# Weight halves that GpSimd's DMAs read twice from DRAM, and a fifth seven-product pair in six units

## The chip, the cores and the metric

The kernel runs on one core of one Trainium2 chip. The metric is device time in microseconds (us). The kernel before takes 2133.17 us, the median of three runs (2133.06 to 2133.46). TensorE is called PE here, VectorE DVE, ScalarE ACT, GpSimd POOL and SyncE SP.

## The reference

Two layers of a decoder trunk on 256 tokens of width 2048, in float32:

```python
h = rms_norm(x, attn_norm)
proj = einsum('bsd,de->bse', h, w_in)          # 2048 x 6160, split into eight parts
o_gla = gated linear attention, chunks of 64, per-head norm, times silu(gate)
o_sb  = stick-breaking attention on normalised q, k, per-head norm
x = x + einsum('bse,ed->bsd', concat(o_gla, o_sb), w_o)       # 2048 x 2048
up = square(relu(einsum('bsd,df->bsf', rms_norm(x, mlp_norm), w_up)))   # 2048 x 8192
x = x + einsum('bsf,fd->bsd', up, w_down)                      # 8192 x 2048
```

## The kernel before, in words

Each product of two float32 numbers is made of three matmuls: an operand is split into a rounded high part and the rest, its low part, and `product` adds high x high, high x low and low x high in one PSUM bank. A weight tile is so turned into `whi` (ACT copies it, rounding, L1008) and `wlo` (DVE subtracts `whi` from the raw weights, L1012).

The MLP, the output projection and some columns of the input projection run in `ordered`, which cuts them into *units*. A unit of the kinds in `BIG` (up, down, and three parts of the input projection, iv, ik and iq) multiplies all 2048 rows of its operand by 1024 weight columns. It goes through eight *pairs* j = 0 to 7; a pair is 256 rows of weights, so 2 x 2 blocks of weights against 2 x 2 blocks of activations. There are 38 such units: for each of four quarters q of the hidden width, up with n2 = 0, up with n2 = 1, down with n2 = 0, down with n2 = 1, in each of the two layers, and iv, ik, iq before each layer's attention.

- An ordinary pair takes eight block products, in two steps: (banks 2, 4), then (banks 3, 8), 12 matmuls each.
- A *seven-product* pair (those in `FAST`, 1, 3, 5 and 6) follows Winograd's form of Strassen's method: seven block products, 21 matmuls, in four steps with the banks (2, 3), (5, 7), (1, 6) and (4). DVE first makes sums of weight blocks for it (`ts`, then two sums in place in `raw`, all at L840), and four low parts instead of two. Sums of the activation blocks come from `forms`.
- An *added* pair (`ADDED`, 2 and 7) is an ordinary pair whose low parts are not made by DVE: ACT writes the negated, rounded weights into a tile `dlo` (L1018), and a DMA of POOL's adds the raw weights, already in SBUF, to it (L1021). Its high parts are still made by ACT at L1008.

`STEPS` (L22) lists the steps of a unit by their pair; `FEWER` is for the one unit iv that follows a down unit. After the last steps of a unit, `sums` and `half` of `down_tail` or `up_tail` drain its banks on DVE. An up unit with n2 = 0 and q over 0 follows a down unit, so that no transposes stand in its first steps; a unit that follows an up unit has that unit's `turn` there, in the banks 5, 7, 1 and 6.

The raw weights of a pair, 1 MiB, are loaded by SP into one of `RAWS` = 5 tiles (`load`, L981; two loads by columns for pair 7, L976). `whi` has `RING` = 5 tiles, `wlo` `LOWS` = 4, `dlo` `ADDS` = 2.

The order on PE is the order in which `ordered` lists the steps. The order of DVE and ACT is written out ahead of time by `Plan.run`: each piece has a length and a due time, counted back from the PE piece that needs it, and a simulated engine always takes the ready piece that is due first. SP and POOL take their instructions in order. Nothing of that is decided on the chip: an engine waits at the first instruction that is not ready, with all behind it.

```python
STEPS = [0, 0, 1, 1, 1, 2, 3, 1, 3, 2, 3, 3, 4, 4, 5, 5, 6, 5, 5, 6, 6, 6, 7, 7]
FAST = (1, 3, 5, 6)
ADDED = (2, 7)
```

Of the kernel before, what the change touches and what calls it, by code (L numbers as in the profile page):

```python
# [17 lines left out]
P = 128  # L18
# [29 lines left out]
class Plan:  # L48
# [10 lines left out]
    class Piece:  # L59
        def __init__(self, engine, length, fn, deps, lag):  # L60
            self.engine, self.length, self.fn, self.lag = engine, length, fn, lag
            self.deps = deps
            self.users = []
            self.after = []
# [4 lines left out]
    def add(self, engine, length, fn, *deps, lag=0.0):  # L69
        flat = []  # L70
        for d in deps:
            flat.extend(d if isinstance(d, (list, tuple)) else [d])
        self.pieces.append(Plan.Piece(engine, length, fn, [d for d in flat if d], lag))
        return self.pieces[-1]

    def run(self):
# [25 lines left out]
        order, events, count = [], [], 0  # L102
        for p in self.pieces:
            if not p.deps:
                events.append((0.0, count, p))
                count += 1
        came = set()
        while events:
            now, _, p = heapq.heappop(events)
# [6 lines left out]
            for e in free:  # L116
                if free[e] > now + 1e-9:
                    continue
                if e in ready:
                    if not ready[e]:  # L120
                        continue
                    p = heapq.heappop(ready[e])[2]
# [6 lines left out]
                heapq.heappush(events, (free[e], count, None))  # L129
                count += 1  # L130
                for u in p.users:
# [4 lines left out]
                    if not left[u]:  # L136
                        heapq.heappush(events, (at[u], count, u))
# [9 lines left out]
def trunk_kernel(  # L147
# [59 lines left out]

    ATT = ("wg", "ident16", "mask16", "tri", "nones", "gmask", "reset", "v4", "lr", "lrT", "ha", "hh", "hl", "hA", "on", "dec", "S", "kdz", "row", "bc", "eg")
    MLP = ("whi5", "dlo", "sxh", "sx", "ts", "raw2")
# [213 lines left out]
    def forms(op, i, t, tag):  # L423

        keep = tag is None
# [16 lines left out]
        def high():  # L442
            if e:
                if keep:
# [378 lines left out]
    def ordered(l, units, hT, rst, ug, gates_t, mixed=None, ons=None):  # L823
# [11 lines left out]
        RING, LOWS, ADDS, RAWS = 5, 4, 2, 5  # L835
# [11 lines left out]
        def unit_order(u):  # L847

            kind, _, n2 = units[u]
            if kind == "g":  # L850
                return [i // 2 for i in range(8)], ()
            if kind == "o":
                pairs = ((4, 5, 6, 7, 0, 1, 2, 3), (4, 5, 6, 0, 7, 1, 2, 3))[n2]
                return [j for j in pairs for _ in range(4 if j < 2 else 2)], (0, 1)
            return FEWER if u and units[u - 1][0] == "down" and kind == "iv" else (STEPS, FAST)

        def step_banks(u, j, is_fast):
# [4 lines left out]
            if kind in BIG and j in ADDED and not by_columns(u, j):  # L862
# [24 lines left out]
        def squares(n, ss):  # L887
            return add("ACT", 2 * A1, lambda: norm_squares(n, ss), x_done[n])
# [23 lines left out]
        def made(f, got, tag_fast, first):  # L912
# [9 lines left out]
            if tag_fast:  # L922
                e = add("DVE", 1.25, lambda: part(0), first)
            b = add("ACT", A1 * (2 if tag_fast else 1), lambda: part(1), e)
            return add("DVE", 1.1 if tag_fast else V1, lambda: part(2), b)

        def turned(n, h2, m, op, key, ll, sums=False):
# [4 lines left out]
            if sums and fast(i):  # L932
                box = []
                b = add("ACT", A1, lambda: box.append(scaled()), a)
                free[m] = [b]
                return made(
                    lambda: forms(op, i, box[0], None if op is hT else "sxh"), None, True, b
# [23 lines left out]
        def load(u, i):  # L961
# [4 lines left out]
            def fn():  # L966
                if x % RAWS >= RAWS - 2:
                    box.append(tmp("raw2", [P, 2, 1024], bufs=2))
# [5 lines left out]
                if by_columns(u, i):  # L974
                    for c in range(2):
                        nc.sync.dma_start(  # L976
                            dst[:, c, :].rearrange("p (k n) -> p k n", k=2),
                            src[:, :, c * 512 : (c + 1) * 512],
                        )
                else:  # L980
                    nc.sync.dma_start(dst, src)  # L981
# [8 lines left out]
        def by_columns(u, i):  # L990

            return units[u][0] in BIG and i in ADDED and i == unit_order(u)[0][-1]
# [763 lines left out]
```

## Time and profile before

| | |
|---|---|
| median of three runs | 2133.17 us |
| the profiled execution: span | 2131.6 us |
| PE busy | 2123.5 us, 10094 matmuls |
| DVE busy | 1929.5 us (91%) |
| ACT busy | 1535.1 us (72%) |
| POOL busy | 152.1 us |
| HBM read | 405.12 MB |
| DMAs of SP's queue | 407.25 MB |
| DMAs of POOL's queue (the adds) | 79.70 MB |

The profiled execution's span, from the first to the last instruction, lies 1.6 us under the median of the runs; that is what a run has around it. In the rows below, "x" is a count, a tile's name stands as out<-in, and a window is given as start:end in us from the span's start. Busy time of an engine is the union of its instructions' times, and successive instructions of DVE and PE overlap a little in the records, so a sum of means is some per cent above it.

### The profile page before, as it was taken

Reading aid. Unit: us, or ns where it says so; the run is one execution under the profiler, and the core shown is the slowest. Engines: PE = TensorE matmul, PEld = TensorE weight load, DVE = VectorE, ACT = ScalarE, POOL = GpSimd, SP = SyncE. Lnnn points to the kernel's source line nnn. Section 1 sums busy time; section 2 is a strip of 40 time slices with the busy share of each in tenths; the row PEclk is TensorE's granted clock in tenths of the full one; section 3 lists DMA queues with packets and bytes.
Section 4 is the critical chain, followed back from the end, with each engine's and each line's share of the span. In section 5 each row is a group of like instructions: output and inputs, shape, how many; then the busy total and the mean of one; then the engine's idle time right before and its main releaser. Section 6 shows DMA issues by size and latency. Waiting matters only on the chain.

```text
span 2131.6 us, 28370 instructions
## 1 busy us (share of the span) xinstructions
PE 2123.5 (100%) x10094; PEld 1768.9 (83%) x10094; DVE 1929.5 (91%) x2598; ACT 1535.1 (72%) x1989; POOL 152.1 (7%) x210
## 2 busy tenths in 40 slices
PE   9999999999999999999999999999999999999999
PEld 7888888888888888888888888888888888888887
DVE  6988779999999999999998886799999999999998
ACT  7777666777677677677777665667876776776775
POOL 0010000000000000000000100000000000000000
PEclk9999999999999999999999999999999999999999
DMA  8975355688888888878888644657888888888886
GB/s 287 265 203 182 115 198 178 217 242 264 249 247 252 249 256 249 269 237 254 238 260 252 178 138 136 201 186 219 262 234 267 245 261 250 246 254 248 254 252 178
DMA packets 156114, 488.76 MB, mean 229 GB/s; under 512 B 9690, under 2 KB 18466, under 8 KB 155972
## 3 DMA queue, kind: packets, MB, share of 16 engines
q1 hardware_dynamic: 134084, 407.25, 55.9%
q0 software_dynamic: 21888, 79.70, 19.7%
q8 instruction: 79, 1.29, 0.2%
q14 instruction: 63, 0.52, 0.1%
HBM read 405.12 MB, written 2.10 MB: 191 GB/s over the span
## 4 chain that ended last, share of the span: by engine, by line
PE 96%; DVE 2%; ACT 1%; issue 0%; DMA 0%; DVEq 0%; ACTq 0%
PE acc L594 3%; PE acc L596 3%; PE acc L595 3%; DVE wlo L1012 0%; PE ps L1693 0%; PE ps L1686 0%; DVE wlo L577 0%; PE ps L705 0%; PE ps L1643 0%; PE ps L759 0%; PE ps L723 0%; DMA dlo<-raw 0%; DVE t L1548 0%; PE ps L471 0%; PE ps L771 0%
## 5 line engine op out<-in xcount | busy, mean ns | idle before, releaser
L1008 ACT ACTIVATE whi<-raw 128x1024 fp32r<-128x1024 f32 (+1 forms) x847 | 814.9, 976 | 344.5 <-issue 48.2
L1012 DVE TENSOR_TENSOR wlo<-raw,whi 128x1024 fp32r<-128x1024 f32 (+1 forms) x695 | 757.6, 1097 | 88.3 <-ACT whi L1008 76.0
L1021 POOL DMA_DIRECT2D dlo<-raw x152 | 129.4, 852 | 1733.7 <-ACT dlo L1018 921.1
L1008 ACT ACTIVATE whi<-ts 128x1024 fp32r<-128x1024 f32 x159 | 168.6, 1060 | 80.0 <-DVE ts L840 5.8
L1012 DVE TENSOR_TENSOR wlo<-ts,whi 128x1024 fp32r<-128x1024 f32 x159 | 193.9, 1219 | 11.1 <-ACT whi L1008 8.4
L840 DVE TENSOR_TENSOR ts<-raw 128x1024 f32<-128x1024 f32 x159 | 194.0, 1220 | 2.7 <-DMA raw<-in_w_in_dram 0.9
L1018 ACT ACTIVATE dlo<-raw 128x1024 fp32r<-128x1024 f32 x152 | 155.3, 1044 | 3.6 <-PE m__2021_9487 L1122 1.7
L594 PE MATMUL acc<-whi,act 128*128 128x512 f32 (+2 forms) x384 | 141.3, 368 | 0.0
L596 PE MATMUL acc<-whi,act 128*128 128x512 f32 (+2 forms) x384 | 136.9, 356 | 0.0
L595 PE MATMUL acc<-wlo,act 128*128 128x512 f32 (+2 forms) x384 | 136.7, 356 | 0.0
L575 ACT ACTIVATE whi<-raw 128x1024 fp32r<-128x1024 f32 (+2 forms) x98 | 88.5, 908 | 63.7 <-PE acc L596 63.0
L577 DVE TENSOR_TENSOR wlo<-raw,whi 128x1024 fp32r<-128x1024 f32 (+2 forms) x98 | 100.4, 1031 | 33.2 <-ACT whi L575 33.1
L840 DVE TENSOR_TENSOR raw<-raw 128x512 f32<-128x512 f32 x159 | 109.4, 688 | 2.7
L840 DVE TENSOR_TENSOR raw<-ts,raw 128x512 f32<-128x512 f32 x159 | 108.9, 685 | 0.7
L594 PEld LDWEIGHTS acc<-whi,act 128*128 128x128 f32 x384 | 72.6, 189 | 12.3 <-issue 3.4
L596 PEld LDWEIGHTS acc<-whi,act 128*128 128x128 f32 x384 | 72.4, 189 | 10.5
L595 PEld LDWEIGHTS acc<-wlo,act 128*128 128x128 f32 x384 | 72.6, 189 | 8.9 <-DVE wlo L577 0.2
L1213 ACT ACTIVATE act<-act,st 128x512 f32<-128x512 f32 x88 | 60.3, 712 | 25.9 <-DVE act L840 25.9
L456 DVE TENSOR_TENSOR act<-t,act 128x512 fp32r<-128x512 f32 x88 | 59.8, 683 | 0.0
L452 ACT ACTIVATE act<-t 128x512 fp32r<-128x512 f32 x88 | 54.3, 621 | 0.4 <-DVE t L440 0.3
L840 DVE TENSOR_TENSOR xb<-t,xb 128x512 f32<-128x512 f32 x40 | 27.3, 682 | 0.1
L663 DVE TENSOR_REDUCE st<-t 128x4 f32<-128x512 f32 (+1 forms) x36 | 21.8, 619 | 5.7 <-ACT t L662 5.5
(3399 smaller groups left out, 5605.6 us busy)
## 6 DMA issues: line engine op xcount, KB each, us to landing
raw<-in_w_up_dram SPq DMA_DIRECT2D x112, 1024.0 KB, 6.3
raw<-in_w_down_dram SPq DMA_DIRECT2D x112, 1024.0 KB, 6.3
raw<-in_w_in_dram SPq DMA_DIRECT2D x78, 1024.0 KB, 5.5
dlo<-raw POOLq DMA_DIRECT2D x152, 512.0 KB, 6.5
raw<-in_w_o_dram SPq DMA_DIRECT2D x32, 1024.0 KB, 5.1
raw<-in_w_up_dram SPq DMA_DIRECT2D x32, 512.0 KB, 6.7
raw<-in_w_down_dram SPq DMA_DIRECT2D x32, 512.0 KB, 6.5
raw<-in_w_in_dram SPq DMA_DIRECT2D x26, 512.0 KB, 6.4
```

The costliest lines, as they stand in the source:

```text
L456: nc.vector.tensor_tensor(d[:, :, 1, :], src, f32(d[:, :, 0, :]), ALU.subtract)
L575: newest["hi"] = nc.scalar.activation(h, r, AF.Copy).ins
L577: newest["lo"] = nc.vector.tensor_tensor(lo[:, q : q + step, :width], r, f32(h), ALU.subtract).ins
L594: nc.tensor.matmul(o, xh[:, sl], whi[:, j, :width], start=first, stop=False)
L595: nc.tensor.matmul(o, xh[:, sl], wlo[:, j, :width], start=False, stop=False)
L596: st["mm"] = nc.tensor.matmul(o, xl[:, sl], whi[:, j, :width], start=False, stop=last).ins
L840: nc.vector.tensor_tensor(dst, a, b, op)
L1008: nc.scalar.activation(box["h"][:, :n], src(), AF.Copy)
L1012: nc.vector.tensor_tensor(box["l"][:, :n], src(), f32(box["h"][:, :n]), ALU.subtract)
L1018: nc.scalar.activation(box["l"], src(), AF.Copy, scale=-1.0)
L1021: nc.gpsimd.dma_start(f32(box["l"]), src(), accum_op=ALU.add)
L1213: nc.scalar.activation(box[h][:, tt, :], box[h][:, tt, :], AF.Relu if into else AF.Copy, scale=(rr if into else st["rst"])[:, tt : tt + 1],)
```

## The change

It has these parts.

1. An added pair is no longer loaded by SP. For each of its two halves POOL issues a DMA that reads 512 KiB from DRAM and writes it, rounded, into a tile `chi` (three of them); ACT negates `chi` into `dlo`; a second POOL DMA reads the same weights from DRAM again and adds them to `dlo`. ACT's L1008 is left out for these halves. POOL's queue holds cast(i+1) ahead of add(i): `halves` makes the cast one half early (`AHEAD_BY`).
2. The added pairs are 2 and 4 instead of 2 and 7, and their halves stand between the seven-product pairs (`EACH`). No pair is loaded by columns any more in these orders.
3. In the six up units with n2 = 0 and q = 1, 2, 3, `MORE` makes pair 0 a fifth seven-product pair, and the unit begins with it. `forms` keeps both kinds of activation sums for pair 0 of the up units (`TWO_WAYS`).
4. `RAWS` is 3 instead of 5; two raw tiles of the scope are gone.
5. The planner counts the five scratch tiles `t2`: a piece that takes one waits in the plan until one is left (`take`, `sure`, `give`), and two pieces get an edge more.

```diff
-STEPS = [0, 0, 1, 1, 1, 2, 3, 1, 3, 2, 3, 3, 4, 4, 5, 5, 6, 5, 5, 6, 6, 6, 7, 7]
-LOADS = [0, 1, 2, 3, 4, 5, 6, 7]
 FAST = (1, 3, 5, 6)
-FEWER = [0, 0, 1, 1, 1, 2, 3, 1, 3, 2, 3, 3, 4, 4, 5, 5, 6, 6, 6, 6, 7, 7], (1, 3, 6)
-ADDED = (2, 7)
+EACH = [0, 0, 1, 1, 1, 1, 2, 3, 3, 3, 3, 2, 5, 5, 5, 5, 4, 6, 6, 6, 6, 4, 7, 7], FAST, (2, 4)
+FEWER = [0, 0, 1, 1, 1, 1, 2, 3, 3, 3, 3, 2, 5, 5, 4, 6, 6, 6, 6, 4, 7, 7], (1, 3, 6), (2, 4)
+FAST_OF = {"sxh": (0, 1, 3, 5, 6), "sx": FAST}
+TWO_WAYS = (("sxh", 0),)
+MORE = [0, 0, 0, 0, 2, 1, 1, 1, 1, 2, 3, 3, 3, 3, 4, 5, 5, 5, 5, 4, 6, 6, 6, 6, 7, 7], (0, 1, 3, 5, 6), (2, 4)
+OWN = {("up", 0): MORE, ("up", 0, 0): EACH}
+CAST, AHEAD_BY = 3, 1
+RING, LOWS, ADDS, RAWS = 5, 4, 2, 3
...
+                    can = [
+                        r for r in ready[e]
+                        if not r[2].take or left_tiles > 1 or left_tiles and sure + r[2].sure
+                    ]
...
-            return FEWER if u and units[u - 1][0] == "down" and kind == "iv" else (STEPS, FAST)
+            if u and units[u - 1][0] == "down" and kind == "iv":
+                return FEWER
+            return OWN.get((kind, n2, q), OWN.get((kind, n2), EACH))
...
-                if x % RAWS >= RAWS - 2:
-                    box.append(tmp("raw2", [P, 2, 1024], bufs=2))
+                if x % RAWS >= 3:
+                    box.append(tmp("raw2", [P, 2, 1024], bufs=RAWS - 3))
...
+        def rounded(u, j, s):
+            box = {}
+            sl = slice(s * 512, (s + 1) * 512)
+            src = weights(u, j)[:, :, sl] if by_columns(u, j) else weights(u, j)[:, s : s + 1, :]
...
+            def high():
+                box["h"] = tmp("chi", [P, 2, 512], F32R, bufs=CAST)
+                nc.gpsimd.dma_start(flat("h"), src)
+            def negated():
+                box["l"] = tmp("dlo", [P, 2, 512], F32R, bufs=ADDS)
+                nc.scalar.activation(box["l"], f32(box["h"]), AF.Copy, scale=-1.0)
+            def add_weights():
+                nc.gpsimd.dma_start(flat("l"), src, accum_op=ALU.add)
+            users = [[], []]
+            h = add("POOL", 1.0, high, chi[-CAST] if len(chi) >= CAST else [], lag=LAND)
+            chi.append(users[0])
+            if len(late) >= AHEAD_BY:
+                late.pop(0)()
+            got = [box, h, None, users]
+            def rest():
+                m = add("ACT", A2, negated, h, dlo[-ADDS] if len(dlo) >= ADDS else [])
+                dlo.append(users[1])
+                got[2] = add("POOL", 1.0, add_weights, m, lag=ADD)
+            late.append(rest)
+            return got
...
-            def negated():
-                box["l"] = tmp("dlo", [P, 2, 512], F32R, bufs=ADDS)
-                nc.scalar.activation(box["l"], src(), AF.Copy, scale=-1.0)
-            def add_weights():
-                nc.gpsimd.dma_start(f32(box["l"]), src(), accum_op=ALU.add)
-            if by_dma:
-                m = add("ACT", A2, negated, deps, dlo[-ADDS] if len(dlo) >= ADDS else [])
-                lo = add("POOL", 2.7, add_weights, m, lag=ADD)
-                dlo.append([])
-                readers.extend((m, lo))
             h = add("ACT", A2 if n == 2 else A1, high, deps, whi[-RING], last.get("h"))
...
+        def halves(u, k):
+            at = [e[:2] for e in every].index((u, k))
+            for v, i, j, s in every[: at + AHEAD_BY + 1]:
+                if (v, i) not in made_halves:
+                    made_halves[v, i] = rounded(v, j, s)
...
-            raw = {j: load(u, j) for j in loads}
+            raw = {j: load(u, j) for j in dict.fromkeys(order) if j not in by_dma}
...
+                if j in by_dma:
+                    prods = next(running[j])
+                    box, h, lo, users = halves(u, k)
```

More of the change, by code (lines that the diff above doesn't have):

```diff
@@ L1036, in parts @@
+            whi[-1].append(lo)
+            readers.append(lo)
             last["h"] = h
             readers.append(h)
-            return box, h, lo, [whi[-1], (dlo if by_dma else wlo)[-1]]
+            return box, h, lo, [whi[-1], wlo[-1]]
         last = {}
         sums13 = []
+        chi, late, made_halves = [], [], {}
+        every = [
+            (u, k, j, order[:k].count(j))
+            for u in range(len(units))
+            for order, _, by_dma in [unit_order(u)]
+            for k, j in enumerate(order) if j in by_dma
+        ]
@@ L1060, in steps @@
                 return
+            kept = kind in AHEAD or ({"up": "sxh", "down": "sx"}.get(kind), j) in TWO_WAYS
             def ext(i):
```

171 lines of the change are left out of this document (101 added, 70 removed).

## The prediction

> **What bounds the kernel now.** I read the page first, then PE's own waits, then the MLP by units, then the DMA queues, and last the opening and one chain of an added half.
>
> ```profile
> PE 2123.5 (100%) x10094; PEld 1768.9 (83%) x10094; DVE 1929.5 (91%) x2598; ACT 1535.1 (72%) x1989; POOL 152.1 (7%) x210
> ...
> PE 96%; DVE 2%; ACT 1%; issue 0%; DMA 0%; DVEq 0%; ACTq 0%
> ```
>
> PE holds 96% of the chain that ended last. Its waits:
>
> ```profile
> PE ps L544 <- POOL ident masks.py:199: 1.4, 1, 1.4
> PE ps L705 <- DVE act L668: 1.1, 2, 0.5
> PE ps L471 <- DMA xb<-in_x_dram: 0.7, 1, 0.7
> PE m__79_428 L1122 <- DMA dlo<-raw: 0.3, 1, 0.3
> PE m__4043_18997 L1121 <- DVE xb L840: 0.2, 1, 0.2
> ```
>
> In the 38 units PE waits 0.5 us in all. The windows below are whole units: the first unit (iv), the second (ik), then of layer 0 down q=0 n2=1, up q=1 n2=0, up q=1 n2=1 and down q=1 n2=0.
>
> ```profile
> core 0: us, PE busy (x) PEld busy (x) DVE busy (x) ACT busy (x) POOL busy (x), PEclk, DMA share, GB/s
> 34.16:76.98 42.82, 42.31 (x181) 33.32 (x180) 41.10 (x59) 33.85 (x41) 3.85 (x5) 1.00 0.84 246
> 76.98:117.78 40.80, 40.80 (x181) 33.78 (x180) 36.84 (x45) 30.41 (x35) 3.85 (x5) 1.00 0.89 259
> 527.50:568.30 40.80, 40.80 (x182) 33.78 (x181) 38.30 (x45) 27.48 (x29) 3.39 (x5) 1.00 0.86 261
> 568.30:609.10 40.80, 40.80 (x182) 33.78 (x181) 37.01 (x44) 28.08 (x31) 3.86 (x5) 1.00 0.85 256
> 609.10:651.70 42.60, 42.60 (x197) 35.43 (x196) 40.78 (x55) 34.03 (x45) 3.37 (x5) 1.00 0.85 245
> 651.70:694.30 42.60, 42.60 (x197) 35.44 (x196) 41.77 (x56) 33.49 (x43) 2.92 (x5) 1.00 0.84 246
> ```
>
> A unit has 4 x 24 + 4 x 21 = 180 matmuls, and 40.80 / 180 = 0.2267 us each, at a granted clock of 1.00. The units of 42.60 have 16 transposes more. So only fewer matmuls can make the MLP faster, and anything that makes PE wait makes it slower. DVE is close behind: 98% in the last window. The up unit that follows a down unit is where DVE has most room, 37.01 of 40.80.
>
> **The matmuls (part 3).** An ordinary pair has 24 matmuls, a seven-product pair 21. `MORE` has 5 x 21 + 3 x 24 = 177, and there are six such units: 18 x 0.2267 = 4.1 us less on PE. `EACH` has 180 and `FEWER` 183, as before. This is 0.19% of the time; 0.2% (4.3 us) is about what a measurement of this kernel tells from no change.
>
> **What DVE pays for it.** The rows of four units:
>
> ```profile
> L1012 DVE TENSOR_TENSOR wlo<-raw,whi 128x1024 fp32r<-128x1024 f32 x48 | 58.4, 1219 | 6.7 <-ACT whi L1008 6.1
> L1012 DVE TENSOR_TENSOR wlo<-ts,whi 128x1024 fp32r<-128x1024 f32 x17 | 20.7, 1219 | 1.2 <-ACT whi L1008 1.2
> L840 DVE TENSOR_TENSOR ts<-raw 128x1024 f32<-128x1024 f32 x16 | 19.5, 1220 | 0.2
> L840 DVE TENSOR_TENSOR raw<-raw 128x512 f32<-128x512 f32 x16 | 11.0, 688 | 0.3
> L840 DVE TENSOR_TENSOR raw<-ts,raw 128x512 f32<-128x512 f32 x16 | 11.0, 685 | 0.1
> L1012 DVE TENSOR_TENSOR wlo<-raw,whi 128x512 fp32r<-128x512 f32 x16 | 10.9, 684 | 0.0
> ```
>
> A seven-product pair costs 1.22 + 0.69 + 0.69 + 3 x 1.22 + 0.68 = 6.9 us of DVE, an ordinary one 2 x 1.22 = 2.4: 4.5 us more per `MORE` unit, at most, as the records overlap a little. That is 37.01 + 4.5 = 41.5 us of work in 177 x 0.2267 = 40.1 us of PE. Over the four units of a quarter it is 157.9 + 4.5 = 162.4 of 166.1 us, 98%, what the unit at 651.70 already bears without a wait. The missing 1.4 us must come from work done ahead. Four `wlo` tiles, the block sums of the first pair and its load allow about 6 us (7's two low parts 2.4, pair 0's first 1.2, its `ts` and one sum 1.9, the last of pair 6 0.7); the tightest stretch, from step (1, 6) of pair 6 to the last step of pair 0 (57 matmuls, 12.9 us), holds 8 drains and 4 halves at 0.68, pairs 7 and 0: 8.2 + 2.4 + 6.9 = 17.5 us, so 4.6 must be ahead. The down unit before has 2.5 us of room to get there. I take 0.1 us of waiting per unit, 0.6 in all; the ends are 0 and 6 x 1.4 = 8.4. The step (2, 3) that now opens the unit needs bank 3 nine matmuls (2.0 us) after its last use, against one 0.68 us drain: covered, unless DVE is in another instruction. The forms kept twice for pair 0 cost a few 0.3 to 0.7 us instructions once a layer, beside ordinary units.
>
> **ACT and the raw tiles (parts 1 and 4).** L1008 goes for 152 halves, 152 x 1.06 = 160 us of ACT, and the extra pairs add 6 x 1.7:
>
> ```profile
> L1008 ACT ACTIVATE whi<-raw 128x1024 fp32r<-128x1024 f32 x688 | 716.7, 1056 | 267.9 <-issue 7.2 <-PE m__634_2947 L1123 6.8 <-PE m__2667_12497 L1123 6.7
> L1018 ACT ACTIVATE dlo<-raw 128x1024 fp32r<-128x1024 f32 x152 | 155.3, 1044 | 3.6 <-PE m__2021_9487 L1122 1.7 <-PE m__2010_9443 L1122 1.1 <-PE m__1935_9093 L1122 0.4
> L1021 POOL DMA_DIRECT2D dlo<-raw x152 | 129.4, 852 | 1733.7 <-ACT dlo L1018 921.1
> ```
>
> PE never waits for ACT, so this gains nothing by itself. SP loads six pairs a unit, so each of three tiles has 20.4 us for a landing (6.3 to 6.6) and its readers (a pair lasts 4.8 to 5.4 on PE); that leaves over 5 us: nothing. POOL's 152 further DMAs at 0.85 us meet 1733.7 us of idleness; cast(i+1) waits for the same half's end as add(i)'s negation and is issued during it.
>
> **The DMA engines (part 1).** The queues over the whole span:
>
> ```profile
> q1 hardware_dynamic: 134084, 407.25, 55.9%
> q0 software_dynamic: 21888, 79.70, 19.7%
> ```
>
> So a plain MB costs 0.559 x 2131.6 / 407.25 = 2.93 us of all engines, an added MB 5.27. A unit has 8.39 plain and 2.10 added: 35.6 us of 40.8. After: 6.29 plain, 2.10 added and 2.10 cast, which no row shows: 29.5 us plus 6.1 (as plain) to 11.0 (as an add), 35.6 to 40.5. I take plain: a cast reads one stream, like the first row, where the add also reads its destination. The other end is a rival. The Trainium skill, "Collectives: The Full Stack", section "The bandwidth ceiling", says that an accumulating transfer is slower because it reads two sources, not because of the addition; 5.27 against 2.93 agrees, and by it the cast would be plain, 35.6 us.
>
> **One added half against its due.** The nearest to the new chain is pair 7's first half to pair 2's first, at a unit's edge:
>
> ```profile
> L1122 PE MATMUL m__1301_6142<-dlo,act x2: 389/389/389, 690.5 to 691.1; 128*128 128x512 f32 x2
> L1018 ACT ACTIVATE dlo<-raw x2: 1043/1044/1046, 692.8 to 695.5; 128x1024 fp32r<-128x1024 f32 x2
> L1021 POOL DMA_DIRECT2D dlo<-raw x2: 841/848/854, 694.2 to 696.9; - x2
> L1122 PE MATMUL m__1385_6521<-dlo,act x2: 389/389/389, 704.1 to 710.2; 128*128 128x512 f32 x2
> DMA to landing us min/median/max: 6.2/6.4/6.6
> ```
>
> `dlo` is free at 691.5; negated at 692.8, added at 694.2, landed by 700.8, read at 704.1: 3.3 us to spare. In `EACH` and `MORE` the same distance, 54 matmuls (12.2 us), lies between the half i-2 and the half i for both halves of pair 4, so two tight chains a unit instead of one. The cast's 0.52 MB on the same queue, 1.3 us earlier, costs the add up to 1.5 us of that. I take no wait; ends 0 and 76 chains x 0.3 us = 23.
>
> **The opening.** Nothing that the first two casts need is missing at the start, and POOL is free at 1.4 us. The DMA engines are full then:
>
> ```profile
> 1.10 0.29 POOL masks.py:199 TENSOR_SCALAR_AFFINE_SELECT ident<-ident 128x128 f32<-128x128 f32 x1
> 2.32 1.85 SPq L564 DMA_DIRECT2D raw<-in_w_in_dram  x4
> 7.98 2.37 ACT L575 ACTIVATE whi<-raw 128x512 fp32r<-128x512 f32 x4
> 8.90 0.78 PE L594 MATMUL acc<-whi,act 128*128 128x512 f32 x1
> ```
>
> ```profile
> raw<-in_w_in_dram SPq DMA_DIRECT2D x4, 256.0 KB, 5.2
> DMA packets 3593, 9.41 MB, mean 392 GB/s; under 512 B 209, under 2 KB 209, under 8 KB 3591
> ```
>
> The first of the last two rows is for the four loads at 2.32, the other for 9 to 33 us. The first weights land near 7.5, half a us before ACT reads them. Two casts, 1.05 MB at 392 GB/s, are 2.7 us of all engines; if they come first, PE's first matmul at 8.90 slips by 2.7 - 0.5, about 2. Ends 0 (issued later, or in gaps) and 2.7; I take 1.9, as the queue they join holds only SP's first loads. The Trainium skill, "DMA: Bandwidth & Descriptors", section "Queues, rings and completion order", says that an engine takes its queues in turn by packets, so casts would push SP's pieces back though these were issued first; that gives up to the same 2.7. The first unit also lost 42.82 - 40.80 = 2.0 us, 0.3 of it for `dlo`; its casts now come early, so I take 0.4 back (ends 0 and 2.0).
>
> **Sum**, against the profiled span: -4.1 + 0.6 + 1.9 - 0.4 = -2.0, so 2129.6; the median of the runs is 1.6 above its span, so 2131.2 us, 0.1% less. Part 5 moves pieces on DVE and ACT among times at which PE does not wait: nothing.
>
> **Rivals.**
> A. The opening's cover holds and the first unit's 2.0 us go: 2133.2 - 4.1 - 2.0 = 2127.1. For it: the casts are needed only at 44 us; against: nothing holds them back, and the engines are full. 0.20.
> B. Slower: DVE becomes the bound in the `MORE` units. For it: 41.5 in 40.1 us, 17.5 in 12.9; against: 98% is borne now. If the lead at the end of the down unit is under 1 us instead of the 4.6 wanted, each unit waits 1.4 and up to another 0.7 for bank 3: 6 x 2.1 = 12.6, so 2131.2 - 0.6 + 12.6 = 2143.2; more than 2.6 us of waiting in the six makes the change slower than before, more than 6.9 by over 0.2%. 0.17.
> C. The cast costs what an add does: 40.5 us of DMA in 40.1 to 42.6. Then landings slip and the tight chains miss: 76 x 0.5 us = 38, so 2169. 0.09.
> D. The adds alone come late behind the casts, 76 x 0.15 = 11: 2142.6. 0.07.
>
> **How the numbers follow.** My forecast has 0.47. Faster by over 0.2% is A, 0.20; slower by over 0.2% is B, C and D, 0.33; the forecast lies within. The range leaves out C and the far ends of A and B: 2126.5 to 2145; the likeliest case's own is 2129.0 to 2135.
>
> **What would show it.** Right: 7761 matmuls at 0.2267 us, `MORE` units near 40.1 us with DVE over 99%; SP's queue near 328 MB, POOL's near 159 MB, the latter's share near 31%; POOL DMAs before 5 us and the first L594 matmul near 10.8. Wrong: `MORE` units over 41 us with PE waiting for `wlo` or `xb` (B), POOL's share near 39% (C), PE waits for `dlo` or `chi` in the pairs 4 (D), or a first matmul still at 8.9 (A).

## The result and the profile after

The changed kernel takes 2145.61 us (median of four runs, 2144.9 to 2150.33) against 2133.28 us for the kernel before on the same chip: 1.0063 times as long, 95% interval 1.0049 to 1.0078. It is slower by 12.3 us, where the forecast had it 2.0 us faster. The profiled execution has a span of 2144.3 us against 2131.6, so 12.7 us have to be found.

The page of the changed kernel; the lines are its engines, its two large DMA queues and the chain that ended last:

```profile
PE 2124.8 (99%) x10076; PEld 1765.1 (82%) x10076; DVE 1944.5 (91%) x2636; ACT 1403.3 (65%) x1853; POOL 234.5 (11%) x362
...
q1 hardware_dynamic: 103076, 327.55, 44.7%
q0 software_dynamic: 43776, 159.40, 31.6%
...
PE 55%; issue 36%; POOL 5%; DMA 2%; DVE 1%; ACT 1%; POOLq 0%
```

PE has 18 matmuls fewer, ACT 132 us less to do, and POOL's queue moves twice the bytes in 31.6% of the engines' time; at the prediction's prices, 5.27 us for an added MB and 2.93 for a plain one, it would be 30.5% if a cast cost what a plain load does. POOL now has 5% of the chain, where it had none. What PE waited for (total, times, longest, in us):

```profile
PE acc L613 <- ACT whi L594: 2.6, 1, 2.6
PE ps L563 <- POOL ident masks.py:199: 2.5, 1, 2.5
PE ps L334 <- DMA t<-in_attn_norm_dram: 2.4, 1, 2.4
PE m__3833_18093 L1199 <- DMA dlo<-in_w_up_dram: 1.2, 1, 1.2
...
PE m__156_800 L1199 <- DMA dlo<-in_w_in_dram: 0.9, 1, 0.9
...
PE m__2637_12424 L1199 <- DVE wlo L1070: 0.8, 1, 0.8
```

The first three stand in the opening. Cut at the first matmul of each unit, the two traces differ as follows (after less before, in us, worked out from the matmuls' starts):

```
opening, up to the first unit                  +8.0
first two units, iv and ik                     +0.6  +1.2
the g unit that opens each layer               +0.9  +0.8
the six MORE units         five times -0.68, once -0.35
the last unit                                  -0.4
all other units                                +5.3
```

The windows show the opening and two of the units, up q=1 n2=0 of layer 0 (a `MORE` unit) and up q=3 n2=1 of layer 1. The columns are window, length, busy us and count of PE, PEld, DVE, ACT and POOL, granted clock, DMA share, GB/s. First the kernel before, then the changed one:

```profile
5.00:10.00 5.00, 5.00 (x21) 4.27 (x20) 2.41 (x6) 3.41 (x8) 0.00 (x0) 1.00 0.88 292
10.00:15.00 5.00, 5.00 (x27) 4.24 (x26) 3.03 (x7) 3.04 (x8) 0.00 (x0) 1.00 1.04 390
15.00:20.00 5.00, 5.00 (x28) 4.22 (x27) 4.59 (x8) 5.00 (x13) 0.00 (x0) 1.00 1.05 397
```

```profile
5.00:10.00 5.00, 2.59 (x16) 2.32 (x15) 0.19 (x1) 1.06 (x1) 0.37 (x1) 0.91 1.03 308
10.00:15.00 5.00, 2.37 (x8) 1.53 (x8) 1.98 (x5) 4.17 (x9) 1.95 (x3) 0.50 1.07 370
15.00:20.00 5.00, 5.00 (x17) 3.89 (x17) 2.17 (x4) 1.24 (x3) 0.00 (x0) 0.56 1.09 310
...
580.24:620.36 40.12, 40.12 (x179) 33.22 (x177) 38.25 (x46) 24.98 (x28) 5.63 (x8) 1.00 0.91 255
...
2012.47:2056.58 44.11, 42.90 (x197) 35.36 (x196) 42.00 (x57) 31.63 (x40) 5.63 (x8) 1.00 0.82 251
```

The `MORE` unit runs without a wait at 40.12 us, with DVE busy for 38.25. The opening shows two losses: PE is idle for half of 5 to 15 us, and after that its clock is granted at 0.50 and 0.56, so that 17 matmuls fit where 28 did. Its timeline (start, length, engine, line; in brackets the idle time before and what ended it):

```profile
1.36 0.69 POOL L1033 DMA_DIRECT2D chi<-in_w_in_dram  x1 [0.33 <-issue]
...
2.14 0.32 POOL masks.py:199 TENSOR_SCALAR_AFFINE_SELECT ident<-ident 128x128 f32<-128x128 f32 x1
...
8.27 1.06 ACT L1037 ACTIVATE dlo<-chi 128x1024 fp32r<-128x1024 f32 x1 [6.16 <-DMA chi<-in_w_in_dram]
...
8.47 0.24 PE L334 MATMUL ps<-ident,t 32*128 32x32 f32 x1 [2.41 <-DMA t<-in_attn_norm_dram]
...
8.75 0.19 DVE L335 COPY gcol_a<-ps 128x32 f32<-128x32 f32 x1 [8.75 <-PE ps L334]
...
10.83 1.06 ACT L1037 ACTIVATE dlo<-chi 128x1024 fp32r<-128x1024 f32 x1 [1.51 <-DMA chi<-in_w_in_dram]
...
11.79 1.55 ACT L500 ACTIVATE act<-ps,gcol_a 128x256 fp32r<-128x256 f32 x4
...
13.91 0.79 PE L613 MATMUL acc<-whi,act 128*128 128x512 f32 x1 [2.63 <-ACT whi L594]
...
24.01 1.09 PE L490 MATMUL ps<-ident,xb 128*128 128x128 f32 x8 [0.81 <-DMA xb<-in_x_dram]
```

The first cast goes out at 1.36 us, ahead of POOL's last instruction for `ident`; the norm's gains `t` land behind the casts, so PE starts `gcol_a` at 8.47. Then `gcol_a` is there at 8.94, but ACT stands in its order at the second negation until the second cast has landed, and takes up `act<-ps,gcol_a` only at 11.79. Followed matmul by matmul, PE is 0.3 us behind the kernel before when it stops for the gains: 1.1 were lost at `ident`, but the wait of 0.7 for x that came next in the kernel before falls away. It is 2.5 behind when the gains are there, 2.0 after the transposes that follow, 5.0 at the first L613 matmul, for which ACT was late, 7.0 when the half clock ends, at 19.4 us (the step of 2.0 is (28 - 17) / 28 x 5), and 8.0 after a wait of 0.8 for x at 24.01, which the kernel before does not have there.

The Trainium skill, "TensorE: Matmul & The Clock Gate", section "Part 1: The HAM clock gate", says that the clock falls to half after about 3.4 us of idleness and comes back after as long a busy stretch. The rows agree in kind: PE idle for 5.0 of the 10 us from 5 on, then 0.50 and 0.56, and 1.00 again from 20 us. But no single wait in them is as long as that; a wait of 2.4 us was enough here, and one of 2.2 in a run further on (`open3`).

The g units lose 1.7 us in the same way. ACT takes two negations directly ahead of the `whi` that the unit's first matmuls need; the kernel before made this `whi` at 284.64, before its g unit began at 289.63:

```profile
296.53 1.99 ACT L1037 ACTIVATE dlo<-chi 128x1024 fp32r<-128x1024 f32 x2
298.43 1.04 ACT L1066 ACTIVATE whi<-raw 128x1024 fp32r<-128x1024 f32 x1
```

The late half of up q=3 n2=1, layer 1, POOL's timeline, SP's, and what the add took to land:

```profile
2035.13 0.56 POOL L1033 DMA_DIRECT2D chi<-in_w_down_dram  x1 [5.77 <-PE m__3846_18144 L1200]
2036.04 0.86 POOL L1040 DMA_DIRECT2D dlo<-in_w_up_dram  x1 [0.35 <-ACT dlo L1037]
...
2036.00 12.25 SPq L1002 DMA_DIRECT2D raw<-in_w_down_dram  x3
...
2048.51 0.50 PE L1199 MATMUL m__3833_18093<-dlo,act 128*128 128x512 f32 x1 [1.22 <-DMA dlo<-in_w_up_dram]
```

A cast, a 1 MB load and the add are issued within 0.9 us, and `dlo` is there 12.4 us after the add's issue, too late by 1.2. Over all 152 adds (time from issue to landing, that is until all their data are written, in us), before and after:

```profile
DMA to landing us min/median/max: 4.5/6.5/11.8
```

```profile
DMA to landing us min/median/max: 5.4/9.6/12.4
```

PE's waits of this kind come to 5.0 us in seven places, against 0.5 before. (A wait is counted here, and in the runs below, as the distance between the starts of two matmuls less the usual 0.227; the idle times that the profile gives for the same places add up to 3.8 and 0.3.)

### The profile page after: what moved, and what is told of

It reads as the page before. It is cut to its first block, busy times and chain, and to the rows that moved or that the text cites. A ratio compares the mean times of both kernels' runs of the same rounds, so it can differ in the third digit from the quotient of the medians.

```text
span 2144.3 us, 28255 instructions
## 1 busy us (share of the span) xinstructions
PE 2124.8 (99%) x10076; PEld 1765.1 (82%) x10076; DVE 1944.5 (91%) x2636; ACT 1403.3 (65%) x1853; POOL 234.5 (11%) x362
## 3 DMA queue, kind: packets, MB, share of 16 engines
q1 hardware_dynamic: 103076, 327.55, 44.7%
q0 software_dynamic: 43776, 159.40, 31.6%
## 4 chain that ended last, share of the span: by engine, by line
PE 55%; issue 36%; POOL 5%; DMA 2%; DVE 1%; ACT 1%; POOLq 0%
POOL dlo L1040 3%; PE acc L613 3%; PE acc L615 2%; PE acc L614 2%; POOL chi L1033 2%; DMA dlo<-in_w_up_dram 1%; DMA dlo<-in_w_in_dram 1%; DMA dlo<-in_w_down_dram 1%; PE ps L1780 0%; DVE wlo L596 0%; DMA chi<-in_w_in_dram 0%; PE ps L724 0%; PE ps L1730 0%; PE ps L1773 0%; PE ps L778 0%
## 5 line engine op out<-in xcount | busy, mean ns | idle before, releaser
L1066 ACT ACTIVATE whi<-raw 128x1024 fp32r<-128x1024 f32 (+1 forms) x701 | 653.2, 955 | 364.6 <-DVE raw L858 209.9
L1037 ACT ACTIVATE dlo<-chi 128x1024 fp32r<-128x1024 f32 x152 | 159.9, 1053 | 83.0 <-DMA chi<-in_w_in_dram 13.9
L1066 ACT ACTIVATE whi<-ts 128x1024 fp32r<-128x1024 f32 x165 | 174.4, 1057 | 53.5 <-DVE ts L858 29.2
L858 DVE TENSOR_TENSOR ts<-raw 128x1024 f32<-128x1024 f32 x165 | 200.7, 1216 | 3.9 <-DMA raw<-in_w_down_dram 2.2
L1070 DVE TENSOR_TENSOR wlo<-ts,whi 128x1024 fp32r<-128x1024 f32 x165 | 200.8, 1217 | 0.4 <-PE m__631_2940 L1199 0.2
L613 PE MATMUL acc<-whi,act 128*128 128x512 f32 (+2 forms) x384 | 142.1, 370 | 2.6 <-ACT whi L594 2.6
L1033 POOL DMA_DIRECT2D chi<-in_w_up_dram x64 | 35.4, 555 | 759.2 <-PE m__2836_13416 L1200 142.1
L1033 POOL DMA_DIRECT2D chi<-in_w_down_dram x64 | 35.4, 554 | 524.2 <-PE m__3624_17092 L1200 33.1
L613 PEld LDWEIGHTS acc<-whi,act 128*128 128x128 f32 x384 | 72.9, 190 | 15.3 <-issue 3.4
L1040 POOL DMA_DIRECT2D dlo<-in_w_down_dram x64 | 54.7, 854 | 68.4 <-ACT dlo L1037 66.0
L1040 POOL DMA_DIRECT2D dlo<-in_w_up_dram x64 | 54.8, 856 | 56.7 <-ACT dlo L1037 55.4
```

What stands on the lines that cost most here:

```text
L613: nc.tensor.matmul(o, xh[:, sl], whi[:, j, :width], start=first, stop=False)
L858: nc.vector.tensor_tensor(dst, a, b, op)
L1033: nc.gpsimd.dma_start(flat("h"), src)
L1037: nc.scalar.activation(box["l"], f32(box["h"]), AF.Copy, scale=-1.0)
L1040: nc.gpsimd.dma_start(flat("l"), src, accum_op=ALU.add)
L1066: nc.scalar.activation(box["h"][:, :n], src(), AF.Copy)
```

## The experiments

**The opening: hold the casts, or hold the negations.** Two kernels take one half each of what was seen. `gate` holds the first two casts behind the last operand of the norm (about 24 us) by a one-column copy into their tile:

```diff
                 box["h"] = tmp("chi", [P, 2, 512], F32R, bufs=CAST)
+                if l < 0 and u == 0 and j == 2:
+                    nc.gpsimd.tensor_copy(box["h"][:, 0, 0:1], f32(hT.t[7])[:, 0, 0, 0:1])
```

> The changed kernel, with the first two casts held back: a one-element copy on POOL into chi, from the last operand pair of the opening, stands ahead of each, so they cannot start before about 24 us. Theory (the opening's 8.0 us come from those casts and what follows them): the first up-kind unit starts near 34.2 us again and the time is 2145.6 - 8 = 2137.6, plus or minus 1. Rival (the loss comes from the steady units, and the late opening is only a shift that the first units would lose anyway): 2145 or so.

`neglate` leaves the casts early and holds the first two negations on ACT in the same way:

```diff
                 box["l"] = tmp("dlo", [P, 2, 512], F32R, bufs=ADDS)
+                if l < 0 and u == 0 and j == 2:
+                    nc.scalar.activation(box["l"][:, 0, 0:1], f32(hT.t[7])[:, 0, 0, 0:1], AF.Copy)
```

> The changed kernel, with the casts early as they are, but the first two negations on ACT held back until the last operand pair of the opening (a one-element copy ahead of each), and with them the first two adds. Theory (about half of the opening's loss is ACT standing at the second negation until the second cast has landed at 10.8 us, and the adds' traffic): first L613 matmul near 11 instead of 13.9 us, 2140 to 2142. Rival (all of it is the casts' share of the DMA engines): no change, 2145.6.

`gate` took 2144.97 us (1.0057, 1.0042 to 1.0072): no gain. Its timeline of ACT and its windows say why:

```profile
33.63 1.06 ACT L1039 ACTIVATE dlo<-chi 128x1024 fp32r<-128x1024 f32 x1 [3.66 <-DMA chi<-in_w_in_dram]
```

```profile
30.00:35.00 5.00, 4.00 (x18) 2.99 (x16) 0.00 (x0) 1.06 (x1) 0.01 (x1) 1.00 1.04 346
35.00:40.00 5.00, 1.58 (x3) 1.02 (x4) 2.23 (x2) 4.26 (x6) 1.79 (x2) 0.80 0.86 160
```

Up to 25 us PE is as busy as in the kernel before, but now ACT stands at the negations until the held casts have landed, DVE does nothing from 30 to 35 us, and the clock falls again. The first unit starts at 37.8 us and loses another 3.9. `neglate` took 2141.21 us (1.0038, 1.0024 to 1.0051). Its first L613 matmul starts at 11.3 instead of 13.9 us, its matmuls are 0.23 us apart from 14.5 us on instead of from 20, and its first unit starts at 37.4, 4.8 us sooner than after. So what costs most is not the casts' bytes but ACT standing in order at an instruction whose data come late, with the slow clock behind it; the bytes keep some 3 us. (The first two adds follow the negations and so are later here too; what their bytes cost was not tested by itself.)

`open2` holds pair 2's casts behind the first operand (7 us), pair 4's behind the eighth, and the negations as `neglate` does. `open3` moves the former to the fifth operand (18 us), and from layer 0 on lets a layer's first two negations wait in the plan for a PE piece shortly ahead of their use:

```diff
+                if l < 0 and u == 0:
+                    nc.gpsimd.tensor_copy(
+                        box["h"][:, 0, 0:1], f32(hT.t[4 if j == 2 else 7])[:, 0, 0, 0:1]
+                    )
                 nc.gpsimd.dma_start(flat("h"), src)
...
-                m = add("ACT", A2, negated, h, dlo[-ADDS] if len(dlo) >= ADDS else [])
+                first = [q for q in plan.pieces if q.engine == "PE"][-30:-29]
+                m = add("ACT", A2, negated, h,
+                        dlo[-ADDS] if len(dlo) >= ADDS else first if l >= 0 else [])
```

> The changed kernel with the first unit's first two casts behind the first operand pair of the opening (about 7 us), its other casts and the first two negations behind the last pair (about 24 us). Theory (the opening's loss is the casts in the first 8 us, plus ACT standing at negations): the first unit starts within 1 us of 34.2, and the time is 2145.6 - 8 + 1 = 2136.5 to 2139, the late adds of the steady units still in it. Rival (1 MB of early reading costs the same wherever it stands in the full queues): 2141 as with the negations alone held back.

> The changed kernel with three bounds on early work: the first unit's casts of pair 2 wait for the norm's fifth transposed form (about 18 us), its casts of pair 4 and the first two negations for the eighth (about 24 us), and from layer 0 on a layer's first two negations wait for the PE piece 30 before, so that ACT doesn't do them at the g unit's start. Theory (the loss is the opening's 8.0 us, 1.7 in the g units and about 5 of late adds): the first unit starts at 34.2 to 35.5 us, the g units' wait for wlo goes (first units of a layer within 0.2 us of before), the waits for dlo of about 5 us stay, the fifth pairs still gain 3.7; 2135 to 2138. Rival (the opening costs because of the bytes, wherever they are put): the first unit still starts 1.5 us late or more, or PE waits for chi in its pairs 2 and 4; 2138.5 or more.

`open2` took 2140.54 us (1.0040, 1.0026 to 1.0054), its first unit starting at 36.1. `open3` took 2138.01 us (1.0025, 1.0016 to 1.0034). Its first unit starts at 33.84 us, 0.3 sooner than in the kernel before, and both g units are within 0.01 us of it. Its windows:

```profile
5.00:10.00 5.00, 4.78 (x23) 3.90 (x22) 2.37 (x6) 3.42 (x8) 0.00 (x0) 1.00 0.90 315
10.00:15.00 5.00, 5.00 (x27) 4.13 (x26) 3.38 (x8) 3.32 (x8) 0.00 (x0) 1.00 1.05 399
```

The same casts, the same bytes and the same negations, only later, cost the opening nothing. With that the 8.0 and the 1.7 us of the g units are explained. By the medians 4.8 us over the kernel before stay, and that with 18 matmuls less. The profiled execution is 3.0 us above its median. In it the first two units lose 2.0, and the units other than these, the six `MORE` units and the last one lose 9.9: 4.7 are waits for late adds (5.3 with one in the second unit), some 1.7 the clock after the longest of them, and 3.5 were not followed. That longest wait, 2.2 us of idle time up to 1949.77 us, cost its unit 4.1 us, as the clock was granted at 0.50 behind it:

```profile
1950.50:1953.90 3.40, 3.40 (x10) 2.66 (x9) 0.00 (x0) 0.05 (x1) 0.00 (x0) 0.50 1.04 341
```

**The fifth pair.** `nomore` is the changed kernel with four seven-product pairs, as before, in the six units; `bmore4` is the kernel before with the fifth pair alone, for which it must give up one of its five raw tiles; `b4` gives up that tile and does nothing else.

```diff
-FAST_OF = {"sxh": (0, 1, 3, 5, 6), "sx": FAST}
-TWO_WAYS = (("sxh", 0),)
-OWN = {("up", 0): MORE, ("up", 0, 0): EACH}
+FAST_OF = {"sxh": FAST, "sx": FAST}
+TWO_WAYS = ()
+OWN = {}
```

> The changed kernel without the fifth seven-product pair: all units but one in the order EACH, 18 matmuls more. Theory (the six units gave 3.7 us as their windows show): 2145.6 + 3.7 = 2149.3. Rival (DVE at 96% in them costs later units as much as they win): 2145.6 or less.

> The kernel before, adds as they were, with the fifth seven-product pair alone in the six up units that follow a down unit (pair 0 first, then the old order), and RAWS 4 instead of 5 to make room for its activation sums. Theory (the fifth pair is worth its 18 matmuls where adds are early): 2133.2 - 4.1 = 2129.1. Rival (98% of DVE and a fourth fewer raw tiles make PE wait): 2133 to 2140.

```diff
-        RING, LOWS, ADDS, RAWS = 5, 4, 2, 5
+        RING, LOWS, ADDS, RAWS = 5, 4, 2, 4
...
-                if x % RAWS >= RAWS - 2:
-                    box.append(tmp("raw2", [P, 2, 1024], bufs=2))
+                if x % RAWS >= 3:
+                    box.append(tmp("raw2", [P, 2, 1024], bufs=RAWS - 3))
```

> The kernel before with RAWS 4 instead of 5 and nothing else. Theory (with four raw tiles an added pair's tile is held until its add has landed, and the loads come late; the 105 us of the run with the fifth pair and RAWS 4 come from this): 2225 to 2240. Rival (the fifth pair overloads DVE and costs them): 2133 to 2140.

`nomore` took 2151.34 us (1.0087, 1.0065 to 1.0110), 5.7 more than after. The intervals of the two overlap, its four runs spread over 9.3 us, and one unit of its profiled execution lost 4.6 us to a late add and the half clock behind it. So it agrees with the 3.7 us that the fifth pairs gain in the six units, and does not show more. `bmore4` took 2238.48 (1.0491), and `b4` 2236.71 (1.0485, 1.0470 to 1.0501): the whole of `bmore4`'s loss is the raw tile that it gives up. In the kernel before an added pair holds its raw tile until both adds have read it, and there four tiles are too few. SP's queue waits for that at the line of its loads 54 times in `b4` (total, times, longest, in us), where it does 5 times and for 11.3 us in the kernel before:

```profile
SPq L981 <- DMA dlo<-raw: 490.0, 54, 17.5
```

Once the adds read DRAM themselves, three are enough. So the two halves of the change hang together: without the first there is no room for the second.

**More tiles.** On `open2`, a fourth cast tile, or a third `dlo`, each paid for with one of the five `whi` tiles:

```diff
-CAST, AHEAD_BY = 3, 1
-RING, LOWS, ADDS, RAWS = 5, 4, 2, 3
+CAST, AHEAD_BY = 4, 1
+RING, LOWS, ADDS, RAWS = 4, 4, 2, 3
```

> The same, with a fourth chi tile (whi has four tiles instead of five, to make room), so that a cast is free to go one half earlier than the add beside it. Theory (adds land late, 9.6 us, because cast, add and raw load are all released by the same half's end): adds land in 8 us or less, the waits for dlo (some 5 us in all) go, 3 to 5 us less than with the opening alone mended, 2132 to 2135. Rival (the engines are full in these stretches, 0.90 to 0.92, and the order doesn't matter): no change in the landing and the time, or more by the smaller whi ring.

```diff
-RING, LOWS, ADDS, RAWS = 5, 4, 2, 3
+RING, LOWS, ADDS, RAWS = 4, 4, 3, 3
```

> The same as the mended opening, with a third dlo tile (whi four tiles instead of five), so that a negation may start one half earlier: 87 matmuls instead of 54 between release and use. Theory (late adds are the steady units' loss): no wait for dlo is left, 4 to 5 us less than with the opening alone mended. Rival (negations that wait in ACT's order for casts that have not landed take the place): same or slower.

They took 2156.69 us (1.0108) and 2254.36 us (1.0567). Adds land in 9.3 us in the first, no sooner; in the second in 7.7, but PE waits for ACT's `whi` in many units:

```profile
PE m__1389_6564 L1204 <- ACT whi L1072: 2.8, 1, 2.8
PE m__2635_12426 L1204 <- ACT whi L1072: 2.7, 1, 2.7
```

The fifth `whi` tile can't be spared, so neither run says what a tile for the adds is worth. `cast4only` takes the room from the fifth pairs instead (`open3` with the edit of `nomore`, and `CAST` 4):

> As open3, with four-product pairs as before in place of the fifth seven-product pair (18 matmuls more), whose kept forms' room goes to a fourth tile for the casts; all else as open3. Theory (what makes an add late is the cast that is released by the same half's end): with a tile more the cast is issued a half earlier, adds land near 8 us, the waits for dlo fall under 2 us; with the 18 matmuls 2136 to 2139.5. Rival (an add is late because of the raw load beside it and of its own two streams, or the cast takes its place in the queue at the same time as before): adds still land near 9.5 us, about 5 us of waits stay; 2140 to 2143.

It took 2143.55 us (1.0043, 1.0026 to 1.0060), adds landing in 9.9 us: the theory fell. A cast that may go a half earlier changes nothing, as in POOL's queue it still goes out directly ahead of an add.

**The order in POOL's queue.** `open3swap` puts the add of a half ahead of the cast of the next:

```diff
+            if len(late) >= AHEAD_BY:
+                late.pop(0)()
             h = add("POOL", 1.0, high, chi[-CAST] if len(chi) >= CAST else [], lag=LAND)
             chi.append(users[0])
-            if len(late) >= AHEAD_BY:
-                late.pop(0)()
```

> As open3, but in POOL's queue the add of a half stands ahead of the cast of the next half. Theory (the adds are late because the cast before them in the queue, the raw load and the add itself are released by the same half's end and share the engines): adds land about 1.5 to 2 us sooner, near 7.5 to 8 us in the median, the waits for dlo fall to under 1.5 us; 2131.5 to 2134, if the casts still come in time. Rival: the cast now stands behind the add's wait for its negation and lands late, ACT stands at the next negation, and PE waits for whi, wlo or dlo in most units; 2140 or more.

It took 2240.55 us (1.0504, 1.0489 to 1.0520). Both came true: the adds land sooner, and the casts, behind the add's wait for its negation, come too late.

```profile
PE m__3142_14871 L1209 <- DMA dlo<-in_w_up_dram: 8.5, 2, 4.8
PE m__3760_17761 L1209 <- DMA dlo<-in_w_up_dram: 7.3, 2, 4.8
```

```profile
DMA to landing us min/median/max: 5.2/7.8/10.4
```

**What stands ahead of an add.** The records of all 152 adds can be sorted by whether a 1 MB load was issued shortly ahead of them. Median time from an add's issue to its first data packets, and to its landing, in us:

```
                                load 0 to 1.5 us ahead    1.5 to 4 us ahead       no load in 4 us
before (no casts)               10: first 5.4, 9.5        58: first 2.2, 6.2      84: first 2.5, 6.5
after, a cast just ahead        79: first 5.2, 10.3       25: first 4.8, 9.9      40: first 2.7, 7.9
open3swap, no cast just ahead   19: first 4.4, 8.9        48: first 2.2, 7.2      27: first 1.7, 5.5
```

A cast ahead costs 1.4 us against the kernel before (7.9 against 6.5), which is what the prediction allowed. But the adds of the kernel before read SBUF. Adds that read DRAM, with neither a cast nor a load ahead, land in 5.5 us in `open3swap`, and against these the cast costs 2.4. A load ahead costs another 2.4 (10.3 against 7.9), and nearly all of it passes before the add's first packet. The kernel before has the same: its ten adds behind a load land in 9.5 us. New is that this is so for 79 adds instead of 10. Behind a cast, a load 1.5 to 4 us ahead costs nearly as much (9.9 against 7.9), where it cost nothing in the kernel before; why was not tested.

The Trainium skill, "DMA: Bandwidth & Descriptors", section "Queues, rings and completion order", says that an engine drains a packet of some 9 to 17 descriptors from one queue before it turns to another. A 1 MB load puts 16 pieces of 4 KB on each engine, and at the 159 ns that one takes in the records that is 2.5 us: the trace agrees for the loads just ahead, with 2.5 us more until the first packet (5.2 against 2.7). The prediction drew on the rule for the opening alone.

`loadlate` tests it: a load that the plan puts from 0.8 us before an add to 2.0 us after it is held until that add is issued, by a one-column write of POOL's into its tile, behind the add (99 loads).

```diff
+                near = [begin[a] for a in adds if -SOONER < begin[a] - begin[p] < LATER]
+                if near:
+                    p.hold = True
+                    rank[p] = max(rank[p], max(near) + 0.01)
...
+                if piece.hold:
+                    nc.gpsimd.memset(dst[:, 0, 0:1], 0.0)
```

> open3, and 1 MB weight loads that the plan puts between 0.8 us before and 2.0 us after an added half's add are held until that add is issued, by a one-column write of GpSimd into their tile behind the add (99 loads). In open3's trace the adds with a load issued 0 to 1.5 us ahead land 10.1 us after their issue, those with no load in the 4 us before 7.8. Theory (an add that is issued just behind a load waits for the load's packets): adds land in 7 to 8 us in the median, the waits for dlo fall from some 5 to 10 us to under 2; 2129 to 2133. Rival 1 (the cast ahead in the same queue makes them late, not the load): adds still land in 9 to 10 us; 2136 to 2140. Rival 2 (the loads have no time to spare): PE waits for wlo or whi behind late raw tiles; 2138 or more.

`castsooner` is `cast4only` with the add moved ahead of the cast and `AHEAD_BY` 2; `castsooner_loadlate` has both edits.

> As cast4only (four-product pairs in place of the fifth ones, four cast tiles), with the cast of the half after the next issued behind each add, instead of the cast of the next half ahead of it. Rival 1 (it is the cast in the queue): adds land in 7 to 8 us, ACT finds its casts landed, PE's waits for dlo go; 2132 to 2135 with 18 matmuls more than open3. Theory (it is the load): adds behind a load still land in 9 us or more, 2136 to 2142. As open3swap's adds landed in 7.8 us with the cast behind them, the truth may lie between: then 2134 to 2137.

> castsooner with the loads held as in loadlate. If both the cast ahead and the load ahead cost an add its time, adds land in 5.5 to 6.5 us, as in the kernel before, and no wait for dlo is left: 2132.5 to 2134, the kernel before's time less nothing, since it has the same matmuls. If held loads come too late: 2136 or more, with PE's waits behind raw tiles.

`castsooner` took 2144.04 us (1.0051, 1.0036 to 1.0066) and says nothing on the cast: in its trace a cast of a later half still goes out 0.9 us ahead of most adds, which land in 10.0 us. But beside it `castsooner_loadlate` differs by the held loads alone, and took 2136.47 us (1.0017, 1.0008 to 1.0027), 7.6 less. Its adds land in 8.9 us and none is waited for; PE's longest waits in the units:

```profile
PE m__83_444 L1228 <- DVE wlo L1099: 0.8, 1, 0.8
PE m__1674_7980 L1227 <- DVE xb L873: 0.7, 1, 0.7
```

It stays 3.4 us above the kernel before, with as many matmuls; 1.2 of it are lost in the first unit.

In `loadlate`, with three cast tiles and the fifth pairs, the adds land sooner too, 8.5 us in the median against `open3`'s 9.5:

```profile
DMA to landing us min/median/max: 5.3/8.5/14.1
```

But the time is the same, 2138.83 us (1.0025, 1.0016 to 1.0035), where 2129 to 2133 was expected, with 7.4 us of waits for `dlo` in six places. Where PE waited longest, at 689.55 us, a load had slipped out 1.3 us ahead of the add, which landed in 11.6; at 1023.53 the negation had begun 2.8 us after its tile was free, as ACT was at other work.

`loadplan` works the plan out again with the held loads in it, so that ACT's order knows of them; `loadplan_cs` does so for `castsooner_loadlate`:

```diff
+                near = [a for a in adds if -1.5 < begin[a] - begin[p] < 2.0]
+                if near:
+                    p.hold = True
+                    p.deps = p.deps + [near[-1]]
```

> As loadlate, but the plan itself knows of the held loads (it is worked out again with each of them behind its add), so that ACT's order no longer has a reader of a held load ahead of a negation, and it holds loads from 1.5 us before an add on. In loadlate negations began up to 2.8 us after their buffer was free and 27 of 152 adds still had a load ahead. Theory (load ahead of the add, and the order that ignored the delay): adds behind a load become rare, adds land near 8 us, waits for dlo under 1.5 us, and the fifth pairs' 3.7 us come out as a gain: 2129.5 to 2133. Rival (the cast ahead in the queue and the wider spread of the packets are enough to be late): waits for dlo of 4 us or more stay: 2135 to 2139.

> castsooner_loadlate (four-product pairs, four cast tiles) with the plan of loadplan. It has no wait for dlo to lose, so by the theory only about 1 us of DVE and first-unit waits can go: 2132.5 to 2136. If the new order costs ACT or DVE something: 2137 or more. Against loadplan it shows what a fourth cast tile is worth against the fifth pairs.

They took 2262.88 us (1.0609) and 2233.83 us (1.0472), a miss of 100 us and more. No wait for `dlo` is left in `loadplan`, but SP's queue stands behind the holds, and PE waits for `whi` and `wlo` in nearly every unit, by the same amount from quarter to quarter:

```profile
SPq L1016 <- POOL raw L1013: 870.1, 130, 11.3
```

```profile
PE m__2821_13446 L1224 <- ACT whi L1092: 6.0, 2, 3.4
...
PE m__1285_6133 L1225 <- DVE wlo L1096: 2.0, 2, 1.2
```

Whether the loads came too late for three tiles, or the new order of DVE and ACT was the worse one, these two runs don't tell apart. None of the kernels tried is faster than the kernel before.

## Why the prediction was wrong

- **The opening** was the term that failed: 1.9 us, ends 0 and 2.7, against 8.0. The step priced the casts as bytes ahead of PE's first matmul. It did not follow what was queued behind the negations on ACT, which now stood at the head of ACT's order with data that land at 10.8 us (3.0 us); nor that the gains `t`, and later a part of x, are as exposed to the casts as the weights (2.2 and 1.0); nor the half clock that follows an idle PE (2.0). `open3`, with the same bytes, lost nothing. The signs named for it, POOL's DMAs before 5 us and a late first matmul, came, at 13.9 instead of 10.8 us.
- **The g units**, 1.7 us, had no term at all. It is the same thing once more, two negations directly ahead of the `whi` that the g unit waits for; `open3`, which lets them wait, is within 0.01 us of the kernel before.
- **The tight chain**: "no wait" was taken, with ends 0 and 23; it was 5.0 us of waits. The cast's 1.5 us were right against the adds of the kernel before (1.4), and too little against adds that read DRAM (2.4); either would have fitted into the 3.3 to spare. What was left out is the load beside them: 2.4 us more, for half of the adds. That the loads count is shown by `castsooner` and `castsooner_loadlate`, which differ in them alone. Rival D had the right place, at 11 instead of 5, and put it down to the casts alone.
- **The first units**: 0.4 back was taken; the first lost 0.6, for which no run shows the cause; the second lost 1.2, most of that at one late add at 119.55 us.
- **The matmuls** were right: -4.1 forecast, -3.7 in the six units. **DVE** too: 0.6 us of waiting was taken, and one of the six is 0.3 us longer than its matmuls, with DVE at 95 to 96% in these units instead of over 99. Rival B did not happen.
- **The DMA engines** were right: 327.55 and 159.40 MB, 31.6% for POOL's queue. Rival C (39%) did not happen. The rule of the Trainium skill cited for it, "Collectives: The Full Stack", section "The bandwidth ceiling", stated there for the reduce step of a collective, agrees in the result: one 4 KB piece of a cast takes 173 to 174 ns in the records, one of a plain load 159, one of an add 327. That it is the second read and not the addition no run here tells apart.
- **The raw tiles**: "nothing" was right for the change as it stands, as no wait for a raw tile came; `b4` shows how wrong it would have been with the adds still reading SBUF.

By the forecast's own sum: -2.0, with 6.1 more for the opening, 1.7 for g, 2.2 for the first two units, 5.3 for the other units (3.9 of it waits for `dlo`), less 0.2 for the `MORE` units and 0.4 for the last, is 12.7, all of it.

## What to carry to other kernels

When a step is moved to where its inputs "miss nothing", look at the engine that has to consume its result: in an order fixed ahead of time, an instruction that is ready later than planned holds everything behind it, and here that and the slow clock behind it cost 4.8 of the opening's 8.0 us, more than the bytes. When three transfers are released by one event, price the last of them behind the other two, from rows in which such a meeting already happens (here ten of the 152 adds of the kernel before). And a change that makes room by a slower path can be worth its cost only together with what it makes room for; test the two apart.

## What was not expected of the hardware

An add that is issued within 1.5 us behind a 1 MB load on another queue starts its data some 2.5 us later than one that isn't (5.2 against 2.7 us in the changed kernel), 16 pieces at 159 ns. An idle PE is paid for twice: in the opening 17 matmuls instead of 28 in the 5 us after it, at a granted clock of 0.56, and in `open3` a clock of 0.50 for 3.4 us behind a wait of 2.2. Not every such wait has it: behind 2.3 us of idle time at 689.55 in `loadlate` the clock stayed at 1.00. And kernels with one and the same set of transfers spread over 7 us from run to run (`open3`, 2135.28 to 2142.31; `loadlate`, 2135.14 to 2141.89), where the kernel before spreads over 1.3; that late adds come at other places each time, some with a slow clock behind them, would explain it, but was not shown. `castsooner_loadlate`, where no add is waited for, spreads over 2.8.
